# An encoder block on one core: low parts of q and k behind both casts, five column tiles of w kept, m's sums from step 58, loads of x behind the last transpose

## The chip, the cores and the metric

One Trainium2 chip, one of its cores. The time is device microseconds of one execution, as the median of the runs shown. The engines are TensorE (PE; PEld is its weight load), VectorE (DVE), ScalarE (ACT), GpSimd (POOL) and SyncE (SP), which here issues nearly all transfers.

## What is computed

One layer of a bidirectional encoder on x of 1024 tokens by 1024 columns, in float32. The reference, cut to its core:

```
h = x @ w_in
q_a, k_a, v_a, z_a, q_b, k_b, v_b, z_b = split(h)
y_a = neighborhood_attention(q_a, k_a, v_a, rel_bias)   # 8 heads, 8 x 16 windows on a 16 x 64 grid
y_b = windowed_gqa_with_sink(rope(q_b), rope(k_b), v_b, sink)   # 8 heads, |i - j| <= 128
mixed = concat(y_a * silu(z_a), y_b * silu(z_b))
out = layer_norm(2**0.25 * x + mixed @ w_out)
```

## The kernel before

Every large product is made from float16 pairs: an operand is cast to a high part on ACT, and a low part (operand minus high part) is made on DVE or POOL. Three matmuls (high by high, high by low, low by high) then stand for one. The kernel has four stages.

- **Head of the program.** x is loaded and split, v is computed, and the first six column tiles of w_in (`ORDER[:NPRO]`) are projected. All 15 later column tiles are loaded once as `ws` (512 KB each) so that `sum_w` can sum their magnitudes for one common scale. `w_scan` sums the magnitudes of an early tile's half, and the small matmul of `w_scale` (L266) then needs that sum. The last `NR` = 8 of the 15 tiles stay in SBUF after their sum and are used from there; the others are loaded again in halves as `wr` (256 KB, `w_load`, L229).
- **The steps.** 128 units (group, head, 128 queries) go through a software pipeline, one unit started per step. A unit is scored on PE (`stage_qk`, L858 and L859), its minimum taken on DVE (`sn`, `nm`, L868), its exponential taken on ACT (L883), split into high and low parts (ACT L893, DVE L894), transposed by a DMA that SP issues (`tr`, L897), and multiplied by v on PE four units at a time (`stage_pv`, L923). DVE divides (`on`, L935), PE transposes back (L946) and DVE multiplies the result by the gate into `z` (L949, L952). Between these, PE works through a list, `fill`: the other 15 projections (L428), then the first pieces of the output product (L1149). A projection's result for q or k leaves its PSUM bank `ps_pj` by `split_q` or `split_k`: for each of two heads a cast on ACT (L298) and a low part on DVE (L304). PE may write the bank again when both low parts are done. The low parts `wl` of the weight tiles, the copies of k and the scaling of the bias tiles (one every eight steps) are POOL's.
- **Preparing the output product.** Its sub-blocks are combined as in one level of Strassen's scheme for the first two row blocks: sums S1 to S4 of the gated outputs (`m_queue`: sums in place in `z`, L1108, and parts `m` and `A`, casts L1086 and low parts L1089) and sums of w_out (`t_prep`, stored to DRAM as `td` and loaded back as `T0` to `T3`). w_out's plain parts are `wob` loads and `wo` parts (`b_load`, `b_split`; L1058, L996, L998, L999). The lists `M_AT`, `B_LD` and `B_AT` give the step at which each is queued, `M_KEYS` and `B_KEYS` which. `pop` and `fill_in` issue queued work when a bookkeeping of due times says that an engine has room.
- **The end, `final`.** `m_last` casts and splits the last two parts of z (`A_3`). Then eight banks of products are added to x, scaled by 2**0.25 (`x_scale`, L1179; `add`, L1184), with statistics (L1190), and normalized: rows 0, 1, 2, 4, 5, 6 on ACT and POOL, rows 7 and 3 last, on all engines.

Each engine works through its own instructions strictly in the order in which the program issued them, and so does SP's queue of transfers.

Of the kernel before, what the change touches and what calls it, by code (L numbers as in the profile page):

```python
# [33 lines left out]
NR = 8  # L34
# [12 lines left out]
M_AT = [74, 80, 87, 104, 112, 119, 123]  # L47
M_KEYS = (("A11", 0), ("A12", 0)), (("A11", 1), ("A12", 1)), (("A22", 0), ("A22", 1)), (("S3", 0), ("S1", 0)), \
    (("S2", 0), ("S4", 0)), (("S3", 1), ("S1", 1)), (("S2", 1), ("S4", 1))
B_KEYS = [("B11", 0), ("B21", 0), ("B11", 1), ("B21", 1), ("B11", 2), ("B21", 2), ("B11", 3), ("B21", 3),  # L50
          ("B22", 0), ("B22", 1), ("B22", 2), ("B12", 2), ("B22", 3), ("B12", 3)]
B_LD = [62, 64, 66, 70, 72, 82, 84, 86, 92, 97, 104, 108, 111, 113]
B_AT = [75, 77, 79, 81, 90, 92, 97, 99, 102, 107, 117, 118, 119, 120]
T_GO = 38
POOL_Q, DVE_FROM = 2, 112
# [11 lines left out]
def hybrid_block(ctx, tc, xT, x, wt, wv, wo, bias, sink, gain, lbias, cos, sin, bmask, out):  # L67
# [126 lines left out]
    def pop(eng, n, top=1, same=False):  # L194
# [3 lines left out]
            and (eng != "sp" or d.fin + 1.0 < at_step(clock["step"])) for d in op.deps)]  # L198
# [4 lines left out]
    def fill_in(eng):  # L203
        now = at_step(clock["step"])
        if eng == "pool" and sum(op.prio <= 1 for op in queues["pool"]) > POOL_Q:
            return
        ready = [op for e in (eng, "any") for op in queues[e] if op.prio > 1 and (e == eng or eng in op.cost)
                 and (eng != "dve" or clock["step"] >= DVE_FROM or "act" in op.cost) and all(
# [109 lines left out]
    def split_q(p, half, src, dep=None):  # L318
        col = dep is None
        ops = []  # L320
        prio = 0 if dep is None else 1
        eng = "pool" if dep and clock["step"] is not None else "dve"
        for j in range(2):
# [4 lines left out]
            o1 = enq("act", hi, dep, prio=prio, after=28 if dep else 0)  # L328
            ops.append(enq(eng, lo, o1, prio=prio, after=32 if dep else 0))
# [3 lines left out]
    def split_k(p, half, src, dep=None):  # L333
        col = dep is None
        ops = []
        prio = 0 if dep is None else 1
        eng = "pool" if dep and clock["step"] is not None else "dve"
        for j in range(2):
# [9 lines left out]
            o1 = enq("act", hi, dep, prio=prio, after=28 if dep else 0)  # L348
            o2 = enq(eng, lo, o1, prio=prio, after=32 if dep else 0)
# [104 lines left out]
    with ExitStack() as vctx:  # L454
# [311 lines left out]
        for i in range(NS):  # L766
            at(14 + 14 * i, sum_w, i)
# [285 lines left out]
    def b_split(n):  # L1053
# [7 lines left out]
        assert len(t_low) == 8  # L1061
        deps = t_low if n < 4 else t_ops if n in (8, 9) else m_ops[3] + m_ops[4] if n >= 10 else []
        if n in (4, 6):
            b_tile[n] = big_tile(f"wo{n}", (128, 2, 2, 512), F16)
# [6 lines left out]
    def b_home(n):  # L1071
        if n == 0:
            pair_of(rawp.tile([128, 4, 2, 512], F16, tag="raw", name="wo0"), *B_KEYS[:4])
        elif n in (4, 6):
            pair_of(b_tile[n], *B_KEYS[n:n + 2])
        elif n in (8, 9):
            pair_of(rawp.tile([128, 1, 2, 512], F16, tag="hl", name=f"wo{n}", bufs=2), B_KEYS[n])
        elif n in (10, 12):
            t = zslot(f"wo{n}", {10: "zd", 12: "z"}[n]).bitcast(F16)
            pair_of(t.rearrange("p (i h c) -> p i h c", i=2, h=2), *B_KEYS[n:n + 2])  # L1080

    def m_split(key, src, *deps, prio=2, home=None):
# [6 lines left out]
        done[key] = [enq("any", lambda eng: on_eng[eng].tensor_sub(part[key][1], src, part[key][0]), o, prio=prio, cost=SUM)]  # L1089
# [406 lines left out]
```

## Time and profile before

| what | value |
|---|---|
| median of 3 runs | 457.18 us (455.61 to 457.68) |
| the profiled execution | 457.78 us, of which the span from first to last instruction is 456.0 |
| PE busy | 437.1 us |
| DVE, ACT, POOL busy | 339.4, 314.2, 273.2 us |
| DMA | 78.54 MB, mean 172 GB/s |

In the profile's rows of time, the first number is the start in microseconds from the span's start, the second the duration; then follow engine, line, operation, tiles and count. In square brackets stands the time that the engine sat idle just before, and what ended it. A row with a count covers several instructions in a row, and then its second number runs from the first's start to the last's end. Waits are given as total, number of times, longest. DMA shares are a mean over 16 engines and can pass 1. The steps take from about 123 us to 376 us; `final` follows.

### The profile page before, as it was taken

Reading aid. Unit: us, or ns where it says so; the run is one execution under the profiler, and the core shown is the slowest. Engines: PE = TensorE matmul, PEld = TensorE weight load, DVE = VectorE, ACT = ScalarE, POOL = GpSimd, SP = SyncE. Lnnn points to the kernel's source line nnn. Section 1 sums busy time; section 2 is a strip of 40 time slices with the busy share of each in tenths; the row PEclk is TensorE's granted clock in tenths of the full one; section 3 lists DMA queues with packets and bytes.
Section 4 is the critical chain, followed back from the end, with each engine's and each line's share of the span. In section 5 each row is a group of like instructions: output and inputs, shape, how many; then the busy total and the mean of one; then the engine's idle time right before and its main releaser. Section 6 shows DMA issues by size and latency. Waiting matters only on the chain.

```text
span 456.0 us, 9321 instructions
## 1 busy us (share of the span) xinstructions
PE 437.1 (96%) x3205; PEld 251.0 (55%) x3205; DVE 339.4 (74%) x827; ACT 314.2 (69%) x660; POOL 273.2 (60%) x291
## 2 busy tenths in 40 slices
PE   9999999999999999999999999999989978999984
PEld 8997744444455555555554555555545643444433
DVE  6978868339978788886877876877878766575446
ACT  5849788666599898878877777877789854132311
POOL 0200154638658359778836646977989992058572
PEclk9999999999999999999999999999999998999999
DMA  8911679980269999653796999479699999311113
GB/s 279 403 56 55 211 218 325 246 297 27 84 144 207 209 203 190 139 94 89 153 165 158 219 225 185 104 180 195 146 159 259 154 214 393 135 46 70 69 70 116
DMA packets 127951, 78.54 MB, mean 172 GB/s; under 512 B 97184, under 2 KB 106272, under 8 KB 127904
## 3 DMA queue, kind: packets, MB, share of 16 engines
q1 hardware_dynamic: 127760, 77.82, 71.2%
q8 instruction: 25, 0.41, 0.4%
q14 instruction: 22, 0.18, 0.1%
q10 hardware_dynamic: 144, 0.13, 0.1%
HBM read 46.44 MB, written 8.42 MB: 120 GB/s over the span
## 4 chain that ended last, share of the span: by engine, by line
PE 45%; POOL 15%; DVE 12%; issue 11%; ACT 11%; DMA 5%; SPq 1%; POOLq 0%; DVEq 0%; ACTq 0%
PE ps_pj L428 15%; PE ps_s L1149 8%; PE ps_s L535 6%; ACT split L893 3%; PE ps_pj L535 3%; PE ps_t L535 3%; POOL wl L246 3%; PE ps_pj L1149 3%; DVE split L894 2%; ACT ps_s L883 2%; POOL m L1089 2%; DVE ks L304 2%; PE ps_t L923 2%; PE ps_t L1149 2%; DMA ws<-in_wt 2%
## 5 line engine op out<-in xcount | busy, mean ns | idle before, releaser
L428 PE MATMUL ps_pj<-xf,wh 128*128 128x512 f16 x672 | 201.3, 379 | 2.6 <-DVE qs L304 1.9
L428 PE MATMUL ps_pj<-xf,wl 128*128 128x512 f16 x336 | 127.3, 379 | 0.0
L894 DVE SCALAR_TENSOR_TENSOR split<-ps_s,split 128x384 f16<-128x384 f32 (+1 forms) x128 | 66.8, 522 | 43.8 <-ACT split L893 41.9
L428 PEld LDWEIGHTS <-wh 128*128 128x128 f16 x672 | 63.0, 98 | 64.9 <-DVE qs L304 2.9
L883 ACT ACTIVATE ps_s<-sn,nm 128x385 f32<-128x385 f32 (+3 forms) x128 | 70.9, 554 | 25.7 <-DVE nm L868 25.1
L245 POOL TENSOR_SCALAR wr<-wr,wsc 128x512 f32<-128x512 f32 x26 | 20.6, 791 | 67.6 <-ACT wh L240 50.2
L893 ACT ACTIVATE split<-ps_s 128x384 f16<-128x384 f32 (+1 forms) x128 | 58.4, 456 | 1.8
L428 PEld LDWEIGHTS <-wl 128*128 128x128 f16 x336 | 32.8, 98 | 38.3
L858 PE MATMUL ps_s<-ks,qs 128*128 128x384 f16 (+2 forms) x128 | 39.6, 310 | 1.4 <-DVE split L894 0.9
L868 DVE CUSTOM_DVE_ANT_0 sn<-ps_s,bm,nsk 128x384 f32<-128x384 f32 (+1 forms) x64 | 40.6, 635 | 0.4 <-PE ps_s L859 0.2
L859 PE MATMUL ps_s<-ks,qs 128*128 128x384 f16 (+2 forms) x128 | 39.7, 310 | 0.0
L923 PEld LDWEIGHTS <-tr 128*128 128x128 f16 (+1 forms) x1056 | 36.6, 98 | 5.2 <-DMA tr<-split 2.6
L868 DVE CUSTOM_DVE_ANT_0 sn<-ps_s,bias,sg 128x368 f32<-128x368 f32 (+1 forms) x64 | 36.2, 565 | 2.7 <-PE ps_s L859 2.0
L246 POOL TENSOR_TENSOR wl<-wr,wh 128x512 f16<-128x512 f32 x26 | 32.7, 1257 | 2.2
L1149 PEld LDWEIGHTS <-A 128*128 128x128 f16 x216 | 20.1, 98 | 21.0 <-issue 0.5
L1149 PEld LDWEIGHTS <-m 128*128 128x128 f16 x180 | 17.4, 100 | 22.6 <-issue 5.4
L346 POOL COPY ks<-ks 64x512 f16<-64x512 f16 x40 | 26.0, 662 | 4.8 <-DVE ks L306 1.2
L245 POOL TENSOR_SCALAR ws<-ws,wsc 128x512 f32<-128x512 f32 x16 | 11.1, 695 | 27.1 <-PE ps_s L859 14.2
L1184 DVE SCALAR_TENSOR_TENSOR xr<-ps_s,yc,xr 128x512 f32<-128x512 f32 (+1 forms) x22 | 16.0, 727 | 15.3 <-PE ps_s L1149 14.8
L1252 ACT ACTIVATE xr<-xr,nmr,rstd 128x1024 f32<-128x1024 f32 x6 | 7.4, 1240 | 27.0 <-POOL nmr L1203 27.0
L1149 PE MATMUL ps_s<-T,m 128*128 128x512 f16 x84 | 20.1, 379 | 3.0 <-DVE xr L1184 3.0
L1254 POOL TENSOR_TENSOR xr<-xr,gb 128x512 f32<-128x512 f32 x13 | 16.5, 1271 | 10.2 <-ACT xr L1252 8.1
(208 smaller groups left out, 907.3 us busy)
## 6 DMA issues: line engine op xcount, KB each, us to landing
ws<-in_wt SPq DMA_DIRECT2D x15, 512.0 KB, 7.1
wr<-in_wt SPq DMA_DIRECT2D x26, 256.0 KB, 3.9
wor<-in_wo SPq DMA_DIRECT2D x20, 256.0 KB, 3.9
xr<-in_x SPq DMA_DIRECT2D x8, 512.0 KB, 9.3
out<-xr SPq DMA_DIRECT2D x15, 256.0 KB, 2.0
wob<-in_wo SPq DMA_DIRECT2D x14, 256.0 KB, 4.2
bias<-in_bias SPq DMA_DIRECT2D x8, 440.0 KB, 4.2
wvraw<-in_wv SPq DMA_DIRECT2D x9, 320.0 KB, 5.6
```

The source lines that it names most:

```text
L245: nc.gpsimd.tensor_scalar(raw, raw, scale, 1.0, op0=ALU.mult, op1=ALU.mult)
L246: nc.gpsimd.tensor_sub(l, raw, h)
L428: nc.tensor.matmul(ps, a[:, k % 4, :], mv, start=(k == 0 and i == 0), stop=(k == KT - 1 and i == 2))
L535: nc.tensor.matmul(ps[:, :320], lh[:, ts], rh[:, cs], start=(k == ko[0] and i == 0), stop=(k == ko[-1] and i == 2))
L858: nc.tensor.matmul(ps[:, :n], q, sl[0], start=True, stop=False)
L859: nc.tensor.matmul(ps[:, :n], q, sl[1], start=False, stop=True)
L868: nc.vector.tensor_tensor_reduce(sn[:, :n], ps[:, :n], bias_t, sg[:, c:c + 1], init, op0=ALU.add, op1=ALU.min, accum_out=nm)
L883: nc.scalar.activation(pt[:, :m], sn[:, :m], AF.Exp, bias=nm, scale=-1.0, accum_out=acc)
L893: nc.scalar.activation(hl[:, :m, 0, :], src, AF.Copy, scale=PSCALE)
L894: nc.vector.scalar_tensor_tensor(hl[:, :m, 1, :], src, PSCALE, hl[:, :m, 0, :], op0=ALU.mult, op1=ALU.subtract)
L923: nc.tensor.matmul(ps[:, w * m:w * m + e], a, b_, start=(i == 0), stop=(i == len(mms) - 1))
L1149: nc.tensor.matmul(ps[:, cs], lh[:, 128 * t:128 * t + 128], rh[:, cs], start=(fresh and e == 0 and n == 0), stop=(e == len(terms) - 1 and ...
```

## The change

Five things are done.

1. In `split_q` and `split_k` both casts are issued first and both low parts after them, and outside the roped heads each low part depends on both casts. A second `pop("dve", 1, 0, same=True)` lets two low parts go in one step.
2. `NR` is 5, not 8. Three column tiles more are loaded again in halves, which is 6 more `wr` loads of 256 KB; in SP's order they stand among the transposes of units 30 to 51. The slots of the three tiles become free after their sums.
3. `m_queue` starts at step 58, not 74, in another order of parts, and w_out's B parts are queued in another order: (B11, 2), (B21, 2), (B11, 3), (B21, 3) are now the last four of 14. Three S sums and their parts are issued to POOL some 65 rows earlier.
4. In SP's queue x's first row block and T0 no longer stand among the last transposes, and in `final` x's row 0 is scaled and added before the last A parts; the low part of A12 is fixed to DVE, that of A22 to POOL. For t = 3, `add(7, 1, b[3])` comes before the product `d`, not after it.
5. `sum_w(11)` comes 8 matmuls later, behind a `w_scan`; `wo_scale` waits for a step divisible by 4; DVE may take added work in steps 112 to 123 only; in `pop`, ACT's work with a dependency on POOL waits for POOL's due time.

```diff
-NR = 8
+NR = 5
-M_AT = [74, 80, 87, 104, 112, 119, 123]
+M_AT = [58, 62, 66, 87, 95, 104, 123]
-B_AT = [75, 77, 79, 81, 90, 92, 97, 99, 102, 107, 117, 118, 119, 120]
+B_AT = [75, 77, 79, 81, 84, 88, 97, 99, 103, 107, 111, 112, 118, 119]
-POOL_Q, DVE_FROM = 2, 112
+POOL_Q, DVE_ADD = 2, range(112, 124)
...
-            o1 = enq("act", hi, dep, prio=prio, after=28 if dep else 0)
-            ops.append(enq(eng, lo, o1, prio=prio, after=32 if dep else 0))
+            high.append((enq("act", hi, dep, prio=prio, after=28 if dep else 0), lo))
+        for j, (o1, lo) in enumerate(high):
+            ops.append(enq(eng, lo, *([o1] if dep else [h[0] for h in high]), prio=prio, after=32 if dep else 0))
...
-            at(14 + 14 * i, sum_w, i)
+            at(14 + 14 * i + (8 if i == 11 else 0), sum_w, i)
...
         x_load(5)
         x_load(2)
+        x_scale(0)
+        a, b = ([obank.get((name, t)) for t in range(4)] for name in ("q2", "q1"))
+        add(0, 0, b[0])
         m_last()
...
-        for t in (0, 4, 1):
+        for t in (4, 1):
             x_scale(t)
...
                 a[3] = run("q2", 3, bank("pj"), (0, 1))
                 run("q7", t, b[t])
+                add(7, 1, b[3])
                 d = run("d", t, bank("pj"))
-            add(4 + t, 1, d)
-            add(4 + t, 1, b[t], whole=True)
+            add(4 + t, 1, d, whole=t == 3)
+            if t < 3:
+                add(4 + t, 1, b[t], whole=True)
...
-        for n, sl in (("A12", ZL), ("A22", ZH)):
-            m_split((n, 3), z[:, sl])
+        for n, sl, eng in (("A12", ZL, "dve"), ("A22", ZH, "pool")):
+            m_split((n, 3), z[:, sl], low={eng: SUM[eng]})
...
-        if i >= T_GO and len(scans) == 16 and all(op.step is not None and op.fin + 3 < at_step(i) for op in scans):
+        if i >= T_GO and i % 4 == 0 and len(scans) == 16 and all(op.step is not None and op.fin + 3 < at_step(i) for op in scans):
...
-        if i == 125:
+        if i == 129:
+            t_soon(0)
             x_soon(0)
-        if i == 127:
-            t_soon(0)
-        if i == 129:
             t_soon(3)
...
         pop("dve", ND, same=True)
+        pop("dve", 1, 0, same=True)
```

The order of PE's instructions is the same before and after, but for the one small matmul of `wo_scale`.

SP's queue at the end of the steps, before (split_1136 to split_1133 hold units 124 to 127, so the last two transposes are those of units 126 and 127; T_5402 is T0, xr_5330 is x's row 0):

```order
L897 DMA_TRANSPOSE tr<-split_1135 128x6x128
L1039 DMA xr_5330<-in_x 128x1024
L897 DMA_TRANSPOSE tr<-split_1136 128x6x128
L897 DMA_TRANSPOSE tr<-split_1137 128x6x128
L1029 DMA T_5402<-td 128x2x1024
L897 DMA_TRANSPOSE tr<-split_1132 128x6x128
L897 DMA_TRANSPOSE tr<-split_1133 128x4x128
L1029 DMA T_5430<-td 128x2x1024
L1039 DMA xr_5432<-in_x 128x1024
```

And now (T_5456 is T0, xr_5458 x's row 0, T_5460 T3):

```order
L900 DMA_TRANSPOSE tr<-split_1135 128x6x128
L900 DMA_TRANSPOSE tr<-split_1136 128x6x128
L900 DMA_TRANSPOSE tr<-split_1137 128x6x128
L900 DMA_TRANSPOSE tr<-split_1132 128x6x128
L900 DMA_TRANSPOSE tr<-split_1133 128x4x128
L1032 DMA T_5456<-td 128x2x1024
L1042 DMA xr_5458<-in_x 128x1024
L1032 DMA T_5460<-td 128x2x1024
L1042 DMA xr_5469<-in_x 128x1024
```

The two loads have moved from among the last transposes to behind them.

DVE from the last split (unit 127) to its first addition of `final`, before:

```order
L894 SCALAR_TENSOR_TENSOR split_1133<-ps_s,split_1133 128x2x128
L1108 TENSOR_TENSOR z_1815<-z_2825,z_1815 128x512
L1108 TENSOR_TENSOR z_2825<-z_2825,z_1815 128x512
L932 RECIPROCAL ri<-ps_t 128x4
L935 TENSOR_TENSOR on<-ps_t,ri 128x4x64
L996 SCALAR_TENSOR_TENSOR wo_5492<-wob_5209,wsn,wo_5492 128x512
L952 SCALAR_TENSOR_TENSOR z_5086<-ps_t,zc,z_5086 128x16x32
...
L1089 TENSOR_TENSOR m_5169<-z_1815,m_5169 128x512
L1089 TENSOR_TENSOR m_5293<-z_2825,m_5293 128x512
L952 SCALAR_TENSOR_TENSOR z_5086<-ps_t,zc,z_5086 128x16x32
L1089 TENSOR_TENSOR A_3_5591<-z_5086,A_3_5591 128x512
L1184 SCALAR_TENSOR_TENSOR xr_5330<-ps_s,yc,xr_5330 128x512
```

And now:

```order
L897 SCALAR_TENSOR_TENSOR split_1133<-ps_s,split_1133 128x2x128
L935 RECIPROCAL ri<-ps_t 128x4
L938 TENSOR_TENSOR on<-ps_t,ri 128x4x64
L955 SCALAR_TENSOR_TENSOR z_5118<-ps_t,zc,z_5118 128x16x32
...
L955 SCALAR_TENSOR_TENSOR z_5118<-ps_t,zc,z_5118 128x16x32
L1172 MEMSET eps 128x1
L1186 SCALAR_TENSOR_TENSOR xr_5458<-ps_s,yc,xr_5458 128x512
L1091 TENSOR_TENSOR A_3_5604<-z_5118,A_3_5604 128x512
```

The two sums in z, a part of w_out and two parts of m are no longer DVE's, and the first addition stands ahead of the last A part.

POOL behind the last scaling of a bias tile, before (A_2 and A_3 are low parts of A; a wob row and the wo row behind it make one low part of w_out):

```order
L833 TENSOR_SCALAR bias<-bias,rsg 128x880
L1089 TENSOR_TENSOR A_2_5059<-z_1049,A_2_5059 128x512
L1089 TENSOR_TENSOR A_2_5079<-z_1475,A_2_5079 128x512
L998 TENSOR_SCALAR wob_4915<-wob_4915,wsn 128x512
L999 TENSOR_TENSOR wo_4444<-wob_4915,wo_4444 128x512
L998 TENSOR_SCALAR wob_4961<-wob_4961,wsn 128x512
L999 TENSOR_TENSOR wo_5162<-wob_4961,wo_5162 128x512
L1089 TENSOR_TENSOR m_4672<-z_923,m_4672 128x512
```

And now (wo_4943 holds B11 and B21 of row block 2, wo_5181 those of row block 3):

```order
L836 TENSOR_SCALAR bias<-bias,rsg 128x880
L1091 TENSOR_TENSOR A_2_5089<-z_1049,A_2_5089 128x512
L1091 TENSOR_TENSOR A_2_5111<-z_1475,A_2_5111 128x512
L1110 TENSOR_TENSOR z_1815<-z_1815 128x512
L1001 TENSOR_SCALAR wob_4964<-wob_4964,wsn 128x512
L1002 TENSOR_TENSOR wo_4979<-wob_4964,wo_4979 128x512
L1001 TENSOR_SCALAR wob_4990<-wob_4990,wsn 128x512
L1002 TENSOR_TENSOR wo_4943<-wob_4990,wo_4943 128x512
L1001 TENSOR_SCALAR wob_5074<-wob_5074,wsn 128x512
L1002 TENSOR_TENSOR wo_5181<-wob_5074,wo_5181 128x512
L1001 TENSOR_SCALAR wob_5097<-wob_5097,wsn 128x512
L1002 TENSOR_TENSOR wo_5181<-wob_5097,wo_5181 128x512
```

The low part of (B11, 2) is now POOL's sixth and seventh row behind this bias tile. Between the sixth and the eighth bias tile POOL now has eight low parts of w_out where it had seven, and one sum in z less.

More of the change, by code (lines that the diff above doesn't have):

```diff
@@ L319, in split_q @@
         col = dep is None
-        ops = []
+        ops, high = [], []
         prio = 0 if dep is None else 1
@@ L1270, in run @@
             return ps
-        a, b = ([obank.get((name, t)) for t in range(4)] for name in ("q2", "q1"))
         c01 = [run("q5", t, bank("t")) for t in range(2)]
-        add(0, 0, b[0])
         for t in range(4):
```

44 lines of the change are left out of this document (23 added, 21 removed).

## The prediction

> **What bounds the kernel now.** I read the page's busy times first.
>
> ```profile
> PE 437.1 (96%) x3205; PEld 251.0 (55%) x3205; DVE 339.4 (74%) x827; ACT 314.2 (69%) x660; POOL 273.2 (60%) x291
> ```
>
> PE is busy for 437.1 of 456.0 us, and the change leaves its work as it is. So whatever the change can bring lies in PE's 18.9 idle us, and in time that PE counts as busy at a low clock. Next the waits of PE, longest first.
>
> ```profile
> PE ps_s L1149 <- DVE xr L1184: 3.0, 2, 1.6
> PE ps_t L923 <- DMA tr<-split: 2.4, 2, 1.8
> PE ps_t L1221 <- ACT dr L1219: 2.1, 1, 2.1
> PE ps_pj L428 <- DVE qs L304: 1.9, 2, 1.6
> PE ps_t L266 <- ACT junk L260: 1.0, 1, 1.0
> ...
> PE ps_t L782 <- DVE z L949: 0.7, 1, 0.7
> PE ps_pj L428 <- DVE ks L304: 0.7, 3, 0.3
> PE ps_t L946 <- DVE on L935: 0.6, 1, 0.6
> ```
>
> Two places matter: the passage from the steps to `final` (1.8 on a transpose, 0.6 on `on`, 1.4 of the first row's 3.0), and the last row block (1.6 of that 3.0). The wait on `dr` is in the last normalization, which the change leaves alone. Third, PE's clock where those waits are (the columns behind PE, PEld, DVE, ACT and POOL are granted clock, DMA share, GB/s).
>
> ```profile
> 372.00:376.20 4.20, 1.86 (x36) 1.73 (x37) 2.05 (x3) 0.47 (x1) 4.03 (x5) 0.94 1.08 252
> 376.20:380.20 4.00, 4.00 (x18) 1.71 (x17) 2.81 (x4) 0.00 (x0) 2.01 (x2) 0.64 0.98 361
> ```
>
> Behind the wait the clock falls. In work lost that is 4.2 × 0.06 + 4.0 × 0.36 = 1.7 us, which no list of waits shows.
>
> **The head of the program: −1.0 us.** The matmul L266 waits 1.0 us for `w_scan`, which stands behind a sum of a `ws` tile.
>
> ```profile
> 98.04 1.04 ACT L753 ACTIVATE junk<-ws 128x1024 bf16<-128x1024 f32 x1
> ```
>
> That is this sum. Now the scan takes its place at 98.04 and comes at least 1.04 earlier, which covers the wait. Bounds: −1.0, and 0 if the scan's own load is late or the microsecond is lost again before the steps. I take −1.0: in the list, no other wait belongs to this stage.
>
> **The matmul of `wo_scale`: −0.7 us.** It waits 0.7 for a `ps_t` bank that a product with z holds. A step divisible by 4 is the one just ahead of that use of the bank, so the bank is free. Bounds −0.7 and 0.
>
> **Casts before low parts: −0.6 us.** ACT's second cast waited for DVE's first low part.
>
> ```profile
> ACT qs L298 <- DVE qs L304: 7.0, 8, 1.1
> ACT ks L298 <- DVE ks L304: 4.5, 6, 0.9
> ```
>
> These 11.5 us of ACT go. What PE waits for is the end of the second low part, though. Its costliest case:
>
> ```profile
> 330.55 0.59 ACT L298 ACTIVATE qs<-ps_pj 64x512 f16<-64x512 f32 x1 [0.94 <-DVE qs L304]
> 332.42 0.56 DVE L894 SCALAR_TENSOR_TENSOR split<-ps_s,split 128x384 f16<-128x384 f32 x1 [1.27 <-ACT split L893]
> 333.01 0.69 DVE L304 SCALAR_TENSOR_TENSOR qs<-ps_pj,qs 64x512 f16<-64x512 f32 x1
> ```
>
> The second cast starts 0.94 earlier, and so do ACT's split behind it and DVE's split (331.5 instead of 332.42). But then DVE makes two low parts of 0.69 where it made one: it ends 0.94 − 0.69 = 0.3 earlier. Of the 1.9 + 0.7 = 2.6 us of PE's waits on low parts I take −0.6: this 0.3, and as much from the four small ones. Bounds: −2.6, and +11 (the rival below).
>
> **POOL at the first pieces of the output product: +0.8 us.** What is moved or added early costs nothing. These are the stretch with the 6 loads, and that with m's first sums:
>
> ```profile
> 182.00:222.00 40.00, 39.29 (x347) 22.23 (x344) 32.09 (x97) 33.40 (x86) 32.60 (x34) 1.00 0.54 104
> 236.00:276.00 40.00, 38.65 (x336) 21.60 (x334) 31.59 (x87) 30.56 (x66) 23.22 (x29) 1.00 0.98 194
> ```
>
> DMA is half free in the first (0.54), POOL in the second (23.2 of 40 us, and the casts find ACT at 30.6). Without that cover the loads would hold SP's transposes for 6 × 0.6 us, and about seven rows of 1.2 us would hold POOL's weight parts. Late in the steps there is no room, and what PE needs first has moved to the end of POOL's list.
>
> ```profile
> 349.45 1.01 POOL L833 TENSOR_SCALAR bias<-bias,rsg 128x880 f32<-128x880 f32 x1
> 350.41 2.28 POOL L1089 TENSOR_TENSOR A<-z,A 128x512 f16<-128x512 f32 x2
> 358.26 0.81 PE L1149 MATMUL ps_pj<-wo,A 128*128 128x512 f16 x3
> ```
>
> The groups between 317 and 379 us give the prices:
>
> ```profile
> L999 POOL TENSOR_TENSOR wo<-wob,wo 128x512 f16<-128x512 f32 x11 | 13.1, 1188 | 0.9
> ...
> L998 POOL TENSOR_SCALAR wob<-wob,wsn 128x512 f32<-128x512 f32 x11 | 9.5, 862 | 0.0
> ```
>
> A low part of w_out is 0.86 + 1.19 = 2.05; a sum in z, of the same shape, I price as an A part, 1.1. Up to this bias tile POOL has one more of the first and one less of the second, +0.9: the tile ends at 350.46 + 0.9 = 351.4. Then two A parts 2.3, a sum 1.1 and two low parts 4.1: (B11, 2) is ready at 358.9. PE's matmuls on it start at 358.26, and the second of them reads the low part at 358.5. The step waits 0.4, and PE may come 0.3 to 0.6 earlier than before. I take +0.8. Bounds: 0, and +4.0 if each of ten pairs takes as long as the slowest here.
>
> **From the steps to `final`: −5.5 us.** In SP's queue the last transposes were late. DVE's last split ends at 368.43, and its transpose is issued last of these:
>
> ```profile
> 368.01 0.42 DVE L894 SCALAR_TENSOR_TENSOR split<-ps_s,split 128x256 f16<-128x256 f32 x1 [0.64 <-ACT split L893]
> 365.12 0.57 SPq L1039 DMA_DIRECT2D xr<-in_x  x1
> 365.80 4.02 SPq L897 DMA_TRANSPOSE tr<-split  x2
> 369.87 0.58 SPq L1029 DMA_DIRECT2D T<-td  x1
> 370.86 2.55 SPq L897 DMA_TRANSPOSE tr<-split  x2
> 375.53 0.95 PE L923 MATMUL ps_t<-va,tr 128*128 128x65 f16 x15 [1.82 <-DMA tr<-split]
> ```
>
> From 365.12 to 373.41 SP issues four transposes and two loads. Without the loads (0.7 and 1.0 with what lies around them) the last starts at 372.2 − 1.7 = 370.5 at the latest, and at 368.7 if the long 4.02 was the load's doing. It was issued at 372.2, the second half of 370.86 to 373.41, and PE went on at 375.5, so at most 3.3 us to landing: now between 372.0 and 373.8. PE wants it at 375.53 − 1.82 − 0.64 = 373.1. The 1.8 go, all or all but 0.7. The 0.6 go with DVE's two z sums, which stood before `on`:
>
> ```profile
> 368.97 2.85 DVE L1108 TENSOR_TENSOR z<-z,z 128x512 f32<-128x512 f32 x2 [0.53 <-POOL m L1089]
> ...
> 382.64 1.23 DVE L1089 TENSOR_TENSOR A<-z,A 128x512 f16<-128x512 f32 x1 [1.20 <-ACT A L1086]
> 383.80 0.74 DVE L1184 SCALAR_TENSOR_TENSOR xr<-ps_s,yc,xr 128x512 f32<-128x512 f32 x1
> 384.59 1.45 PE L1149 MATMUL ps_s<-T,m 128*128 128x512 f16 x6 [1.35 <-DVE xr L1184]
> ```
>
> The 1.35 before S2's product were A's low part standing ahead of the addition; the order is now the other one, so the addition runs beside PE's 12 matmuls of S1. And with PE at work, the clock's 1.7 us go as well: 1.8 + 0.6 + 1.35 + 1.7 = 5.5. **What is late next** is T0 and x's row 0, now issued behind the transposes, about 370.0 to 372.4.
>
> ```profile
> T<-td SPq DMA_DIRECT2D x1, 512.0 KB, 5.6
> ```
>
> That is T3, issued behind the transposes at 373.46. At 5.6 us T0 lands at 375.6 to 378.0. S2's product would start at 384.59 − 5.5 = 379.1, and S1's 12 matmuls (2.75, as in the last fence below) want T0 at 376.3. x's row 0 lands 1.4 later (512 KB at the 361 GB/s above) and is scaled (1.0, an estimate from ACT's 1.04 for as many columns) and added (0.74) at 378.8 to 381.2. So this is covered in the early case and costs up to 2.1 in the late one. Bounds: −5.5 and, where the transposes do not come earlier at all, −2.0; I take the first, because the issue of the last transpose is bound by the split at 368.43 once nothing stands between.
>
> [...]
>
> **The last row block: −1.6 us.** `p4` waited for `add(7, 1, b[3])`, which stood behind `d` and its addition.
>
> ```profile
> 433.52 2.75 PE L1149 MATMUL ps_pj<-wo,A 128*128 128x512 f16 x12
> 437.09 0.75 DVE L1184 SCALAR_TENSOR_TENSOR xr<-ps_s,yc,xr 128x512 f32<-128x512 f32 x1
> ```
>
> Now those 0.75 us run beside `d`'s 2.75, and the bank is free when `d` ends. PE's 1.6 us go, and what DVE does to the end starts from PE's results, so the end moves as much. Bounds −1.6 and −0.8 (if the added statistics delay DVE by one addition).
>
> **Sum.** −1.0 − 0.7 − 0.6 + 0.8 − 5.5 − 1.6 = −8.6. The profiled execution took 457.78 (span 456.0 and 1.8 around it), 0.6 over the median of the runs shown; I add to it and get **449.2 us**, so the forecast leans high rather than low by this choice.
>
> **Rivals.**
> - *The transposes stay late.* SP was also behind before the loads. Then 1.8 and the 1.7 of the clock stay: 452.7. For it, the 4.02 for two transposes, which the load need not have caused; against it, the two loads that leave SP's queue. 0.14.
> - *POOL takes over between 358 and 365 us.* At its slowest price PE waits 4.0, not 0.8: 452.4, or 454.1 if the clock falls there. For it, POOL's rows, which follow one another without a pause at 350 us; against it, one low part of w_out and two of m fewer behind that bias tile. 0.12.
> - *The half clock stays though the wait goes*, being set by something else than these waits: 449.2 + 1.7 = 450.9. For it, a longest wait of only 1.82; against it, that the clock falls nowhere else in the steps. 0.08. [...]
> - *More goes at the low parts* and POOL is in time: 449.2 − 2.0 − 0.8 = 446.4. 0.06.
> - *The first two together*, so that the expected gain is mostly turned into new waits: 452.7 + 3.2 = 455.9. 0.05.
> - *Slower: the pair of low parts becomes the bound.* There are 16 such pairs in the steps. Each starts its first low part later by the time to the second cast, and if DVE had no wait there to fill, PE's bank is 0.69 later: 16 × 0.69 = 11.0, 449.2 + 0.6 + 11.0 = 460.8. It decides where ACT's removed wait (11.5 us over 14 casts, 0.82 each) no longer reaches DVE. 0.05.
>
> **Numbers.** The forecast has 0.50, its own range 447.5 to 451.0. The range that leaves out at most 2 in 10 runs from the fourth rival to the upper end of the second: 446.4 to 454.5. A measurement of this kernel tells about 0.5% from no change, 2.3 us: faster is below 454.9, slower above 459.5. Faster takes the forecast and the first four rivals, 0.90, less 0.03 for what no row prices: 0.87. Same is the fifth and 0.02 of that, 0.07; slower the sixth and 0.01, 0.06.
>
> **What would show it.** Right: no PE wait on `tr` near 372 us, a granted clock of 1.0 there, the first addition before the A part and no wait ahead of S2's product, no wait on `xr` L1186 near 430, none at L267; PE starts `final` about 8 us earlier. Wrong: a wait of PE on T0, on x's scaling or on POOL's low parts of w_out, or PE's waits on low parts of q and k grown past 2.6 us.

## The result, and the profile after

The changed kernel takes 451.62 us (median of 4 runs, 450.46 to 452.20) beside 456.39 for the kernel before on the same chip (4 runs, 455.21 to 457.68): a ratio of 0.9892, with an interval of 0.9852 to 0.9931. That is 4.8 us less, where 8.6 us were forecast from a profiled execution of 457.78; the forecast of 449.2 was 2.4 us too low. Four further runs of the changed kernel, with their own runs of before, had a median of 450.84, a ratio of 0.9865 (0.9823 to 0.9907). Single executions vary: 31 of the kernel before lie between 454.2 and 460.8.

The profiled execution of the changed kernel took 452.2 us, with a span of 450.0. Its waits of PE, longest first (total, times, longest):

```profile
PE ps_t L926 <- DMA tr<-split: 2.9, 5, 1.1
PE ps_t L1223 <- ACT dr L1221: 2.7, 1, 2.7
PE ps_pj L431 <- DVE qs L305: 1.4, 1, 1.4
PE ps_pj L1151 <- DVE xr L1186: 1.1, 1, 1.1
...
PE ps_pj L431 <- DVE ks L305: 0.7, 2, 0.5
PE ps_t L267 <- ACT junk L756: 0.6, 1, 0.6
```

The two longest places of before are gone: no wait on `tr` near 372 us (the 2.9 are five short ones, all earlier), none of 1.4 and 1.6 on `xr`. What has come in their place: 1.1 on `xr` ahead of `d`, 0.6 at L267, and 2.7 instead of 2.1 on `dr`. The clock where those waits were (columns as in the prediction: PE, PEld, DVE, ACT, POOL, granted clock, DMA share, GB/s):

```profile
372.00:376.20 4.20, 4.20 (x52) 2.69 (x50) 1.64 (x4) 0.00 (x0) 0.35 (x1) 1.00 0.97 308
376.20:380.20 4.00, 3.98 (x19) 1.71 (x18) 1.83 (x4) 3.12 (x4) 1.29 (x1) 1.00 1.03 403
```

PE's timeline at the first row block of `final`:

```profile
375.72 2.75 PE L1151 MATMUL ps_t<-T,m 128*128 128x512 f16 x12
378.50 1.46 PE L1151 MATMUL ps_s<-T,m 128*128 128x512 f16 x6
379.79 1.46 PE L1151 MATMUL ps_pj<-wo,A 128*128 128x512 f16 x6
382.38 2.75 PE L1151 MATMUL ps_pj<-wo,A 128*128 128x512 f16 x12 [1.14 <-DVE xr L1186]
```

S2's product starts at 378.50, not at 384.59, with no wait ahead of it. `d` then waits 1.14 where it waited 0.20, so it starts 5.2 us earlier than before and not 6.1. The last row block brings another 1.8, and the end gives 1.0 back: the span is 6.0 us shorter.

To compare kernels, I cut the program at five places on PE: **head** ends with the first product of q and k, **steps** with the last (its first matmul), **passage** with the first matmul on T0, **final** with the matmul on `bb` that stands ahead of the last normalization, **end** with the span. The cuts are PE's starts in each trace, in us:

| kernel (trace) | head | steps | passage | final | end | span |
|---|---|---|---|---|---|---|
| before, shown | 122.05 | 243.02 | 15.42 | 67.86 | 7.65 | 456.0 |
| before, second trace | 121.34 | 244.35 | 12.20 | 67.91 | 7.60 | 453.4 |
| changed, shown | 121.83 | 242.97 | 10.92 | 65.67 | 8.61 | 450.0 |
| changed, second trace | 122.43 | 241.74 | 10.92 | 65.63 | 8.08 | 448.8 |
| end only | 121.98 | 243.40 | 11.75 | 65.42 | 8.95 | 451.5 |
| steps only | 121.17 | 241.69 | 12.14 | 67.67 | 7.53 | 450.2 |
| loads only | 123.31 | 244.69 | 13.08 | 68.63 | 7.59 | 457.3 |
| casts only | 122.76 | 242.51 | 11.76 | 67.67 | 7.40 | 452.1 |
| casts and end | 123.27 | 241.35 | 11.74 | 65.18 | 8.66 | 450.2 |
| changed, casts back | 122.33 | 244.32 | 10.93 | 65.42 | 8.10 | 451.1 |
| changed, loads among | 122.26 | 242.52 | 12.53 | 64.56 | 8.43 | 450.3 |
| changed, warm end | 123.35 | 241.59 | 10.93 | 65.34 | 8.09 | 449.3 |
| changed, row 0 reordered | 122.78 | 242.28 | 10.93 | 65.05 | 8.16 | 449.2 |
| the same, one low part on DVE | 122.71 | 239.92 | 10.93 | 65.32 | 8.12 | 447.0 |

From the traces shown, head to end: −0.2, −0.05, −4.5, −2.2, +1.0. The prediction's terms, put in these stages, are −1.0, −0.5, −4.1, −2.95, 0. At first sight the passage came as forecast, and the early gains were lost in the steps. My first theory was that new waits on `tr` had eaten them. The experiments say otherwise.

### The profile page after: what moved, and what is told of

The parts are those of the page before. It is cut to its first block, busy times and chain, and to the rows that moved or that the text cites. A ratio compares the mean times of both kernels' runs of the same rounds, so it can differ in the third digit from the quotient of the medians.

```text
span 450.0 us, 9339 instructions
## 1 busy us (share of the span) xinstructions
PE 435.7 (97%) x3205; PEld 251.6 (56%) x3205; DVE 334.0 (74%) x823; ACT 314.0 (70%) x660; POOL 278.7 (62%) x295
## 4 chain that ended last, share of the span: by engine, by line
PE 58%; ACT 12%; DMA 11%; DVE 8%; issue 7%; POOL 2%; SPq 1%; DVEq 0%; POOLq 0%; ACTq 0%
PE ps_pj L431 22%; PE ps_s L1151 8%; PE ps_s L538 6%; DMA tr<-split 5%; PE ps_pj L1151 4%; PE ps_t L926 4%; PE ps_pj L538 3%; PE ps_t L538 3%; ACT ps_s L886 3%; ACT split L896 3%; PE ps_s L862 2%; PE ps_s L861 2%; DMA ws<-in_wt 2%; DMA vd<-vt 2%; PE ps_t L1151 2%
## 5 line engine op out<-in xcount | busy, mean ns | idle before, releaser
L246 POOL TENSOR_SCALAR wr<-wr,wsc 128x512 f32<-128x512 f32 x32 | 24.8, 774 | 72.4 <-ACT wh L241 60.7
L247 POOL TENSOR_TENSOR wl<-wr,wh 128x512 f16<-128x512 f32 x32 | 39.6, 1239 | 2.7
L241 ACT ACTIVATE wh<-wr,wsc 128x512 f16<-128x512 f32 x32 | 22.8, 713 | 0.8 <-DVE wsc L271 0.7
L538 PEld LDWEIGHTS <-xf 128*128 128x128 f16 x192 | 18.6, 98 | 7.3
L1151 PE MATMUL ps_pj<-wo,A 128*128 128x512 f16 (+1 forms) x96 | 20.9, 359 | 1.1 <-DVE xr L1186 1.1
```

Of the source, the lines that this page charges most:

```text
L247: nc.gpsimd.tensor_sub(l, raw, h)
L538: nc.tensor.matmul(ps[:, :320], lh[:, ts], rh[:, cs], start=(k == ko[0] and i == 0), stop=(k == ko[-1] and i == 2))
L1151: nc.tensor.matmul(ps[:, cs], lh[:, 128 * t:128 * t + 128], rh[:, cs], start=(fresh and e == 0 and n == 0), stop=(e == len(terms) - 1 and ...
```

## The experiments

### Which part carries the gain

**The end alone** (point 4 of the change), on the kernel before; its main lines:

```diff
+        x_scale(0)
...
+        add(0, 0, b[0])
         m_last()
...
+                add(7, 1, b[3])
                 d = run("d", t, bank("pj"))
...
-        if i == 125:
+        if i == 129:
+            t_soon(0)
             x_soon(0)
-        if i == 127:
-            t_soon(0)
-        if i == 129:
             t_soon(3)
```

> Before, with the end of the change alone: T0 and x's row 0 issued behind the last transposes, the first addition ahead of m's last parts, and add(7, 1, b[3]) ahead of d; nothing of the steps is changed. Theory (these parts carry the whole gain, and the early edits brought nothing): 456.4 - 4.7 (passage) - 1.6 (last row block), and up to 1 us given back in the last normalization, 450 to 451, with no PE wait on tr near 372 us and clock 1.0 there. Rival (the transposes come in time only because DVE has no z sums left after step 123 and POOL had its work earlier, so the end needs the edits of the steps): PE still waits 1 us or more on tr or on `on` near 372, 452.5 or more.

Measured: 454.01 us (10 runs) beside 456.49 (31 runs), 0.9938 (0.9907 to 0.9969), so −2.8 by the ratio: about half of the whole. The theory that these parts carry everything falls. The rival's mechanism is there in small: PE waits 0.64 on `on`, as before, because DVE's sums of z still stand ahead of it, but not on `tr`.

**The steps alone**: the changed kernel with these edits taken back, but for the fixed engines of the last A parts, which stay. Its main lines:

```diff
-        x_scale(0)
...
-        add(0, 0, b[0])
         m_last()
...
-                add(7, 1, b[3])
                 d = run("d", t, bank("pj"))
...
+        if i == 125:
+            x_soon(0)
+        if i == 127:
+            t_soon(0)
         if i == 129:
-            t_soon(0)
-            x_soon(0)
             t_soon(3)
```

> The changed kernel with its passage and last row block put back to what they were before: all that the change does in the steps and in the head is left. Theory (the early gains are spent on new waits for tr): PE reaches the last transposes about 0.4 us earlier, PE's waits on tr between 140 and 360 us are 2 to 3 us in sum (0.6 before), and the time is 455.5 to 456.5. Rival (the -1.0, -0.7, -0.6 and +0.8 of the prediction hold, and what is missing is lost in the passage): 454.9 or less, tr waits as before.

Measured: 453.21 us (10 runs), 0.9930 (0.9898 to 0.9961), −3.2. So the edits of the steps are worth as much as those of the end, and my theory is wrong. Its PE waits:

```profile
PE ps_s L1151 <- DVE xr L1186: 2.8, 2, 1.6
...
PE ps_t L926 <- DMA tr<-split: 0.9, 2, 0.8
PE ps_pj L1151 <- POOL wo L1002: 0.8, 1, 0.8
```

On `tr` it waits 0.9 in all: 0.2 in the steps, and 0.8 in the passage, though there T0 and x's row 0 stand among the transposes as before. The 2.9 of the changed kernel's first trace are not what the edits cost.

**Five tiles of w instead of eight, alone:**

```
-NR = 8
+NR = 5
```

> Before, with five column tiles of w kept and not eight, and nothing else: six loads of 256 KB more in the steps. Theory A (the loads stand among the transposes in SP's queue and hold them): PE's waits on tr between 150 and 300 us, 0.3 before, grow to 1.3 to 2.5, and the time is 457.5 to 459. Theory B (the loads are hidden, and the new waits come from the casts and low parts or from the moved additions): those waits stay below 0.6, time 456.4.

Measured: 457.97 us (10 runs), 1.0027 (0.9995 to 1.0059): not told from no change. PE has no wait on `tr` between 150 and 300 us at all, so the loads don't hold the transposes there: the mechanism of theory A falls, though the median lies in its range of times.

**The order of casts and low parts alone**, on the kernel before:

```
-            o1 = enq("act", hi, dep, ...)
-            ops.append(enq(eng, lo, o1, ...))
+            high.append((enq("act", hi, dep, ...), lo))
+        for j, (o1, lo) in enumerate(high):
+            ops.append(enq(eng, lo, *([o1] if dep else [h[0] for h in high]), ...))
...
         pop("dve", ND, same=True)
+        pop("dve", 1, 0, same=True)
```

> Before, with only the low parts of q and k behind the casts of both heads (and the second place where DVE takes one in a step). Theory B (two low parts in a row, 2 x 0.69, hold DVE's split of the attention weights and so its transpose): PE's waits on low parts fall from 2.6 to about 2.1, its waits on tr grow by 1 to 2.3, time 456.5 to 458. Theory A (the loads of w make the new waits on tr): waits on low parts 2.0 to 2.1, tr as before, time 455.9.

Measured: 454.50 us (10 runs), 0.9953 (0.9926 to 0.9980), −2.1. Both expectations undersized it; theory B had the sign wrong. Its waits on low parts of q and k are 1.0 and 1.0, not 1.9 and 0.7, and on `tr` it waits 0.5 in all.

### How much of a trace belongs to the kernel

The prediction summed rows of one execution. Two more traces, of unchanged kernels:

> The kernel before, unchanged, for a second trace of it. Theory (the 1.8 us wait on tr near 372 us and the half clock behind it belong to the kernel): both are there again, 1.6 to 2.0 us and a granted clock near 0.6 in the four microseconds behind. Rival (they belong to the one execution from which the prediction was summed; the same passage in the run with the loads alone waited 1.0 and kept its clock): the wait is 1.2 us or less and the clock 0.95 or more, and the span 1 to 2.5 us under 456.0.

Measured: 455.23 us, span 453.4. PE's timeline in the passage of this second trace of before:

```profile
373.13 0.63 PE L946 MATMUL ps_t<-identf,on 128*128 128x128 f32 x4 [0.64 <-DVE on L935]
373.59 1.65 PE L923 MATMUL ps_t<-va,tr 128*128 128x65 f16 x33
375.08 2.54 PE L1149 MATMUL ps_s<-wo,m 128*128 128x512 f16 x11
...
382.05 1.46 PE L1149 MATMUL ps_s<-T,m 128*128 128x512 f16 x6 [1.40 <-DVE xr L1184]
```

And its clock there:

```profile
376.20:380.20 4.00, 4.00 (x22) 2.10 (x21) 2.25 (x5) 1.32 (x3) 3.92 (x4) 1.00 1.01 379
```

The group of 33 matmuls on `tr` takes 1.65 us, some 0.45 longer than the same group elsewhere (1.19): that is all that is left of the wait of 1.82. The 11 matmuls behind it take 2.54 at full clock. In the trace shown first they were

```profile
376.28 3.93 PE L1149 MATMUL ps_s<-wo,m 128*128 128x512 f16 x11
```

with a granted clock of 0.50 from 376.20 to 379.00. The 0.64 on `on` and the 1.40 ahead of S2's product are there again. So the rival holds: two of the four parts of the prediction's largest term, 1.8 and 1.7, don't come with each execution. Of 31 executions of this kernel 7 have a mean granted clock of 0.994 or less, like the trace shown first (0.994), the others 0.995 to 0.998, like this one (0.997); so a loss of clock of that size is not rare, but where those seven lost it is not known. SP's queue in this trace shows that the transposes were earlier:

```profile
364.89 0.58 SPq L1039 DMA_DIRECT2D xr<-in_x  x1
365.56 3.22 SPq L897 DMA_TRANSPOSE tr<-split  x2
368.83 0.58 SPq L1029 DMA_DIRECT2D T<-td  x1
369.82 2.54 SPq L897 DMA_TRANSPOSE tr<-split  x2
```

Two transposes behind the load take 3.22, where the trace shown had 4.02, and the last pair starts at 369.82, not 370.86, though PE is 0.6 later. Why the same two took longer in one execution is not shown.

> The changed kernel, unchanged, for more runs beside those of before and for a second trace of it. Theory (the waits on tr in the steps, 2.9 us in sum, come with the change): again 2 to 3.5 us between 140 and 360 us, and about 451.5. Rival (they belong to the one execution: the same steps with the old end had 0.2): under 1 us, and a time of 450 to 451.

Measured: the 450.84 us given above, with these waits:

```profile
PE ps_pj L1151 <- DVE xr L1186: 1.3, 1, 1.3
...
PE ps_pj L1151 <- POOL wo L1002: 0.8, 1, 0.8
...
PE ps_t L926 <- DMA tr<-split: 0.6, 2, 0.4
```

On `tr` PE waits 0.6 in all in the steps, not 2.9: the rival holds. The theory does not vanish wholly: in three traces with the steps of before these waits are 0.6 to 1.2 in sum, with a mean of 0.8, in six with the changed steps 0.2 to 2.9, with a mean of 1.5. But the changed steps are the shorter ones all the same: 241.6 to 243.0 in those six, 243.0 to 244.4 in the three, and the means differ by 1.5. The stages of the two second traces, before and then changed, show the gain without those accidents (a row for each of steps, passage, final and end):

```profile
121.34:365.69 244.35, 238.00 (x2050) 133.76 (x2049) 194.45 (x538) 198.59 (x457) 178.32 (x187) 1.00 0.86 170
365.69:377.89 12.20, 11.45 (x113) 6.71 (x112) 9.74 (x19) 6.81 (x13) 11.78 (x11) 1.00 1.05 245
377.89:445.80 67.91, 64.67 (x335) 31.06 (x333) 40.29 (x75) 20.11 (x25) 37.04 (x35) 1.00 0.32 127
445.80:453.40 7.60, 1.75 (x9) 0.93 (x6) 3.79 (x10) 1.36 (x4) 0.77 (x2) 0.84 0.28 105
```

```profile
122.43:364.17 241.74, 237.43 (x2050) 133.74 (x2048) 194.82 (x539) 201.74 (x463) 187.82 (x196) 1.00 0.90 179
364.17:375.09 10.92, 10.92 (x113) 6.71 (x112) 4.40 (x14) 3.69 (x7) 7.61 (x7) 1.00 0.75 168
375.09:440.72 65.63, 64.35 (x335) 31.07 (x333) 39.70 (x71) 20.32 (x25) 35.58 (x33) 1.00 0.38 147
440.72:448.80 8.08, 1.75 (x9) 0.93 (x6) 4.47 (x14) 1.36 (x4) 1.25 (x2) 0.84 0.26 98
```

PE's matmuls in each stage are the same ones; the steps are 2.6 us shorter, the passage 1.3, `final` 2.3, and the end is 0.5 longer.

### Casts, loads and the end, each undone or joined

**Casts and end joined**, both as in the diffs above, on the kernel before:

> Before, with the two parts that were each faster alone, the casts with low parts behind them (454.5) and the end (454.0); w's eight tiles, m's sums and the parts of w_out as before. Theory (the other early edits, the six loads among them, give nothing or cost up to 1): 450.5 to 452, as fast as the whole change. Rival 1 (casts and end remove the same wait on tr, so that they don't add): 453 to 454. Rival 2 (the early moves are needed to have DVE free of z sums and POOL in time at the end): 452.5 or more with the wait of 0.6 on `on`.

Measured: 451.53 us (4 runs), 0.9880 (0.9842 to 0.9918), beside the changed kernel's 0.9865 on the same chip: the two can't be told apart. So the theory holds for the time: the head's order, the step of `wo_scale`, m's early sums, the order of w_out's parts and the five tiles together bring nothing that can be measured in it. Rival 1 is right in one stage: the passage takes 11.75 with the end alone, 11.76 with the casts alone and 11.74 with both. The mechanism of rival 2 is there too, though not its time: DVE's sums of z still stand ahead of `on`.

```profile
372.06 0.63 PE L948 MATMUL ps_t<-identf,on 128*128 128x128 f32 x4 [0.63 <-DVE on L937]
```

So the early edits do bring something: with them and the loads behind the transposes the passage takes 10.92 or 10.93 in all six traces, without them 11.74 or 11.75 in both. They lose about as much again where POOL's low part is late (the 0.8 above), which this kernel doesn't wait for.

The table also shows what the move of the loads does. In the eight traces with T0 and x's row 0 behind the transposes, PE waits for no transpose in the passage. In the six with them among the transposes the passage is 0 to 3.7 us longer than those values, 1.4 in the mean. The kernel with the casts alone is the one trace of the six without such a delay; in two others the casts are in as well, and PE waited 0.77 there (the steps alone) and 1.17 (a run below). So the casts don't take that wait away each time; behind the move it was in none of eight traces.

**The casts undone** in the changed kernel (the diff of the casts alone, reversed):

> The changed kernel with the low parts of q and k where they were before (each behind its own cast, one place in a step for DVE), and all else changed. In the kernels run so far the time from the first to the last product of q and k is 243.0 to 244.7 us with the old order and 241.4 to 243.0 with the new one. Theory (the casts bring about 2 us, more than the 0.6 of the prediction, and 1.3 of them between the 88th and the 96th product): that stretch takes 16.4 to 16.5 us and not 15.2, and the time is 1.5 to 2.5 above the changed kernel's 450.8, 452.3 to 453.3. Rival (the gain was another part's, or the transposes make the difference from run to run): within 0.5 of the changed kernel.

Measured: 452.74 us (4 runs), 0.9904 (0.9871 to 0.9936). That is 1.7 over the changed kernel's median (451.06 of its 8 runs), but the intervals overlap, so the time alone doesn't settle it. The steps take 244.32, against the 241.6 to 243.0 of six traces, but 1.43 of that is one wait on `tr` near 358 us, of the kind that varies from run to run. More telling is the table as a whole: the five traces with the old order of casts have steps of 243.0 to 244.7, the eight with the new one (the last row of the table left aside) 241.4 to 243.0, and the means differ by 1.9. With the 2.1 of the casts alone, the casts are worth about 2 us. But the stretch from the 88th to the 96th product takes 15.15, not 16.4. It takes 16.3 to 16.5 where both the casts and the other early edits (but for the five tiles) are as before, and 15.15 or 15.16 in every trace with either of them: here, too, two edits take away the same time. The longest waits of PE in the steps are now these, and one on `wog`, which the changed kernel doesn't have:

```profile
PE ps_t L924 <- DMA tr<-split: 2.6, 4, 1.4
PE ps_pj L429 <- DVE qs L305: 1.8, 1, 1.8
...
PE ps_pj L429 <- DVE ks L305: 1.0, 4, 0.3
...
PE ps_t L924 <- DVE wog L784: 0.9, 1, 0.9
```

**The loads back among the last transposes**, in the changed kernel:

```diff
+        if i == 125:
+            x_soon(0)
+        if i == 127:
+            t_soon(0)
         if i == 129:
-            t_soon(0)
-            x_soon(0)
             t_soon(3)
```

> The changed kernel with x's row 0 and T0 again issued at steps 125 and 127, among the last transposes; the first addition stays ahead of m's last parts. Theory (with the new order of casts the last transposes are in time anyway, and the half clock near 376 us was one execution's): PE waits 0.8 or less on tr near 372, keeps its clock, and the time is 0 to 1.0 above the changed kernel's 450.8. Rival (the prediction's step: the loads hold the transposes by 1.8, and the half clock of 1.7 follows): 453 or more.

Measured: 452.07 us (4 runs), 0.9887 (0.9850 to 0.9923): 1.0 over the changed kernel's median, and not told from it by the interval. The prediction's step, 453 or more, is not borne out. PE's timeline:

```profile
373.75 0.91 PE L926 MATMUL ps_t<-va,tr 128*128 128x65 f16 x15 [1.17 <-DMA tr<-split]
374.50 2.54 PE L1151 MATMUL ps_s<-wo,m 128*128 128x512 f16 x11
...
382.86 2.75 PE L1151 MATMUL ps_pj<-wo,A 128*128 128x512 f16 x12 [0.21 <-DVE xr L1186]
```

The wait is 1.17, more than my theory allowed and less than the prediction's 1.8; the clock stays at 1.00 (2.54 for the 11 matmuls). And most of what the move of the loads wins on `tr` it loses ahead of `d`: with the loads early, that wait is 0.21, with them late 1.14 and 1.28 in the two traces of the changed kernel. The passage is 1.6 longer, `final` 1.1 shorter.

### The end, and two ways to go on

**Keeping PE at work** while it waits for `dr`:

```diff
             nc.scalar.activation(dn, identf, AF.Copy, scale=nmr)
+            keep, (lh, _), (rh, _) = bank("s"), part["A12", 3], part["B21", 3]
+            for _ in range(11):
+                nc.tensor.matmul(keep, lh[:, :128], rh, start=True, stop=True, skip_group_check=True)
```

> The changed kernel with eleven matmuls of 128x512 more, which nothing reads, in front of the last two, where TensorE waits 2.7 us for dr. Theory (the half clock at the end comes from that wait): the granted clock in the last 6 us is 0.95 or more, the last two groups take 0.67 and 0.59 and not 1.19 and 1.06, and the time is 0.5 to 1.0 less than that of the changed kernel. Rival (the clock falls there for another reason, or DVE and POOL set the end): the groups stay above 1.0 or the time stays within 0.3.

Measured: 451.37 us (4 runs) beside 450.84 for the changed kernel on the same chip: no gain. The last matmuls, in this kernel, in the second trace of the changed one, and in the kernel with casts and end:

```profile
444.58 0.67 PE L1226 MATMUL ps_t<-xr,dr 128*128 128x256 f32 x2 [0.35 <-ACT dr L1221]
```

```profile
444.08 0.67 PE L1223 MATMUL ps_t<-xr,dr 128*128 128x256 f32 x2 [2.71 <-ACT dr L1221]
```

```profile
444.91 1.19 PE L1223 MATMUL ps_t<-xr,dr 128*128 128x256 f32 x2 [2.71 <-ACT dr L1221]
```

With the wait filled the group takes 0.67. With the same wait of 2.71 it takes 0.67 in one trace and 1.19 in the other. So the half clock doesn't follow from the wait each time; that it needs the wait is likely, since the group took 0.67 in all six traces with a wait of 2.15 or less. Here filling it bought nothing that can be measured.

**Row 0 reordered**, to hide `d`'s wait:

```diff
+            if t == 0:
+                add(t, 1, b[t])
             add(4 + t, 1, cb)
-            add(t, 1, b[t])
+            if t > 0:
+                add(t, 1, b[t])
...
+                if t == 0:
+                    run("q7", t, b[t])
                 d = run("d", t, bank("pj"))
-                run("q7", t, b[t])
+                if t > 0:
+                    run("q7", t, b[t])
```

> The changed kernel with two lines of the first row block in another order: add(0, 1, b[0]) ahead of add(4, 1, cb), and the product q7 ahead of d. Theory (d waits 1.0 to 1.3 us for the bank that add(0, 0, a[0]) reads, and q7 needs nothing of it): the wait before d falls under 0.3, time 1.0 less than the changed kernel's, 449.8. Rival (T3 has not landed by then, or the end of the program takes the microsecond back): PE waits for T3, or the time stays within 0.4.

Measured: 451.10 us (4 runs), no less than the changed kernel. PE's timeline:

```profile
379.91 1.46 PE L1151 MATMUL ps_pj<-wo,A 128*128 128x512 f16 x6
382.02 1.47 PE L1151 MATMUL ps_s<-T,m 128*128 128x512 f16 x6 [0.65 <-DMA T<-td]
383.32 2.75 PE L1151 MATMUL ps_pj<-wo,A 128*128 128x512 f16 x12
```

The wait ahead of `d` is gone, and q7 waits 0.65 for T3 instead: the rival. In this stretch the transfers follow one another (379 to 415 GB/s in the windows of 4 us from 376 to 388, at a DMA share of 1.02 to 1.05), and an order of PE's work that wants one earlier meets the next one that is late.

**The same, and the low part of (B11, 2) on DVE:**

```diff
-        b_ops[n] = enq("any", ..., cost=LOW)
+        b_ops[n] = enq("any", ...,
+                       cost={"dve": LOW["dve"]} if n == 10 else LOW)
```

> The same, and the low part of (B11, 2) on DVE, which takes that of (B11, 3) now, so that POOL has it no more when PE's first output pieces need it. Theory (the 0.8 us that POOL was to cost are real: 0.77 in two traces): no wait on POOL and none of 0.5 or more on tr near 357 us, and 0.5 to 0.8 less than with the other order alone, 449.0 to 449.5. Rival (then PE meets the transpose that stands behind, as in the traces where it waited 0.7 to 0.85 on tr there): no gain over the other order alone.

Measured: 450.31 us (6 runs, 448.84 to 452.46), 0.9855 (0.9823 to 0.9888). It is the lowest median of all kernels run, 0.8 under the other order alone, but not told from it or from the changed kernel's. Its trace is clear at the place in question: no wait on POOL, none on `tr` near 357 us, and the stretch from the product of unit 120 to that of unit 127 takes 11.70, as before the change, where the traces of the changed kernel have 12.6 to 12.7.

## Why the prediction was right, and where it was not

The sign, the two places at the end and most mechanisms were right; the time lies 2.4 us over the forecast, inside the wide range of 446.4 to 454.5 and just over the forecast's own 447.5 to 451.0 (the second median, 450.84, is inside). That it came so near is in part luck: the largest term was booked far too high, the casts too low, and the start of 457.78 was 1.1 to 1.5 over the medians of before. From 456.4 the same sum gives 447.8, 3.8 under the first median. By its own steps:

- **Head, −1.0: nothing that can be seen.** In six traces with the old head it ends between 121.3 and 123.3 us, in the eight with the new one between 121.2 and 123.4. The wait for `w_scan`, 0.99 in the trace shown, is 0.19 to 1.58 in the other five. The new head has none there, but in seven of eight traces 0.46 to 0.93 at `w_scale`, the next matmul that wants a sum. The prediction named this bound ("lost again before the steps") and took the other.
- **`wo_scale`, −0.7: the wait is gone** in every trace of the changed kernel, and was 0.7 to 1.0 in those of before.
- **Casts before low parts, −0.6: about −2**, by the kernel with them alone (−2.1) and by the steps of that without them (+2.2 over the mean of six). I looked at PE's waits on low parts alone; those fell by 0.6, from 2.6 to 2.0, with the casts alone. In the trace of the casts alone the passage is shorter as well (11.76), and the stretch from the 88th to the 96th product by 1.3. Which waits make up the rest is not settled. The slower rival, 11 us for pairs of low parts, is excluded.
- **POOL at the first output pieces, +0.8: right**, 0.77 and 0.76 in two traces and 0.9 in the time of the last steps. In the trace shown first it could not be seen, because there PE waited 0.85 on `tr` just ahead of it. "What is moved or added early costs nothing" is neither shown nor refuted: the loads alone made +1.2 within their interval, and the waits on `tr` in the steps are larger by 0.7 us in the mean, less than the spread from trace to trace.
- **From the steps to `final`, −5.5: the step that failed.** It had four parts: 1.8 on `tr`, 0.6 on `on`, 1.35 ahead of S2's product, 1.7 of clock. The 0.6 and the 1.35 are in both traces of before and in none of the changed kernel. The 1.8 was 0.45 in the second trace of before, and the clock did not fall there at all (1.00). The sum had been made against the profiled execution's own time, 457.78, and taken as a forecast for a kernel whose medians in the later comparisons are 456.3 to 456.6: what that execution lost by accident was booked as a gain. Against the second trace, passage and S2's wait are 1.3 + 1.4 = 2.7, less 1.1 for the new wait ahead of `d`: 1.6 where 5.5 were booked. With the mean of the six traces that have the loads among the transposes (1.4 for `tr` and the clock, where the second trace has 0.45) it is about 2.6.
- **What is late next** was named (T0 and x's row 0), and they came in time; x's row 4 was not looked at. DVE waits 1.22 for its scaled copy in the trace shown, with the addition that frees `d`'s bank queued behind: +0.9, the 1.14 ahead of `d` less 0.20.
- **The last row block, −1.6: right** on PE. But the end took 0.5 to 1.0 back, which "the end moves as much" denied. DVE's chain at the end of the changed kernel's first trace:

```profile
436.86 0.95 DVE L1247 SCALAR_TENSOR_TENSOR xr<-xr,mv,gb 128x512 f32<-128x512 f32 x1
...
438.04 1.43 DVE L1251 SCALAR_TENSOR_TENSOR xr<-xr,rstd,bb 128x512 f32<-128x512 f32 x1
439.40 0.74 DVE L1186 SCALAR_TENSOR_TENSOR xr<-ps_pj,yc,xr 128x512 f32<-128x512 f32 x1
```

The same two took 0.75 and 0.74 before:

```profile
443.81 0.75 DVE L1245 SCALAR_TENSOR_TENSOR xr<-xr,mv,gb 128x512 f32<-128x512 f32 x1
...
444.80 0.74 DVE L1249 SCALAR_TENSOR_TENSOR xr<-xr,rstd,bb 128x512 f32<-128x512 f32 x1
```

There POOL had ended its four passes over row 6 at 443.77, just ahead of them. Now DVE's passes start 6.9 us earlier and POOL's only 5.2 (433.42 for 438.59), and they run together:

```profile
437.34 1.59 POOL L1257 TENSOR_TENSOR xr<-xr,bb 128x512 f32<-128x512 f32 x1
439.05 1.56 POOL L1256 TENSOR_TENSOR xr<-xr,gb 128x512 f32<-128x512 f32 x1
440.69 1.26 POOL L1257 TENSOR_TENSOR xr<-xr,bb 128x512 f32<-128x512 f32 x1
```

POOL's passes take 1.59 and 1.56 beside them and 1.26 alone. DVE's 0.9 us stand ahead of the last additions, and all that follows to `dr` waits for these; the wait on `dr` grows by 0.6. The same holds in every trace: the nine with the new end have 0.94 to 0.96 and 1.43 to 1.44 on DVE and two passes of 1.55 to 1.60 on POOL, the five with the old end 0.75 and 0.74, and 1.26 or 1.27. So the new end brings it; that the two engines hold each other up is read from these durations, and no kernel was run with the new end and POOL's passes elsewhere.

Of the rivals, the half clock that stays was right to doubt the step, but not as it was put: the half clock was not there in the second trace of before, so for the kernel it could neither stay nor go. Its argument, a wait of only 1.82, is not settled by the runs: none shows how long a wait must be for the clock to fall, and in the trace shown the clock was 1.00 behind the wait of 2.15 on `dr`.

Three readings of the prediction were off without changing the sum. The stated upper end of the wide range, 454.5, is not the second rival's 454.1. The list of waits does hold one more in the head, 1.0 on `warm`, which lies at 1 us and is the same before and after. And "about 8 us earlier" for the start of `final` doesn't follow from its terms, which make 7.0 up to S2's product; measured were 6.1.

## What to carry to other kernels

Before pricing a wait of a microsecond, ask whether a second execution has it: a wait on a transfer, and a clock that fell behind it, can belong to the run (here 1.82 us and 0.50 in one trace, 0.45 and 1.00 in the other), while waits set by an engine's order (here 0.64 and 1.35 to 1.40) come back within 0.05 us. Two edits that take away the same wait don't add in that place (here the passage took 11.75 and 11.76 us with one of them and 11.74 with both); running each alone, and each alone undone, shows it. A microsecond taken off PE's path near the end counts only as far as the engines that finish the work are moved with it (here the end took 0.5 to 1.0 us back).

## What the runs showed of the hardware

The granted clock fell to 0.50 behind a wait of 1.82 us in one trace of before (376.20 to 379.00 us). It was 1.00 behind waits of 1.40 (the second trace of before) and 1.17 (the loads among the transposes), and behind one of 0.81 (the loads alone) nine matmuls took 2.10 us, as they do at 1.00. At the end, of eight traces in which PE waits 2.71 to 3.00 us for `dr`, three have the group behind it at 1.19 us and five at 0.67, and the six with waits of 0.35 to 2.15 all at 0.67. So whether the clock falls differs from run to run of the same kernel; what decides it is not shown.

DVE's passes with both inputs in SBUF took 0.95 and 1.43 us beside POOL's and 0.75 and 0.74 without, and POOL's 1.6 beside DVE's and 1.27 without; DVE's additions that read one input from PSUM kept 0.74 beside POOL (439.40). Why is not shown.
